# Backward state products by high and low parts, norm sums in two passes, four PSUM banks for the scan's products and one for the heads'

## The chip, the cores and the metric

One core of a Trainium2 chip. The time is that of one execution on the device, in microseconds; lower is better. The kernel before takes 2713.92 us (median of three runs, 2713.1 to 2715.24). All times below are of the kernel before.

## The reference

An encoder layer for two sequences, of 512 and 1024 tokens, laid end to end here as T = 1536. A normalised and modulated input `h` is multiplied by one wide matrix; one part of the result feeds an attention branch, the other a state-space scan that runs over the tokens in both directions; the two branches are gated, merged and projected. Everything is float32. What the change touches is the scan and the group norms:

```python
proj = h @ w_in                      # 1024 -> 8960
q = rms_norm(q_c, q_a_norm) @ w_q_up # q_c: 384 wide, kv_c: 256 wide
xbc = silu(dwconv_centred(xbc, conv_w, conv_b))
y = ssd(xs, dt_f, A_f, B, C) + flip(ssd(flip(xs), flip(dt_b), A_b, flip(B), flip(C)))
y = rms_norm_of_4_groups(y * silu(z), ssm_norm) @ w_proj_b
# ssd, per chunk of 128 tokens, 4 groups of 8 heads of 64:
y_diag = einsum(C B^T, decay between tokens, x * dt)
states = einsum(B, decay to the chunk's end, x * dt)     # 128 x 512 per group and chunk
h_next = exp(a_last) * h + states                        # over chunks, in both directions
y_off  = einsum(C, h, decay from the chunk's start)
```

## The kernel before

**Products in parts.** A product of float32 operands is made in one of two ways. Either both operands go to TensorE as they are ("fp32"; the trace then has two records for each instruction), or each operand is split in a high part (a cast to float32r on ScalarE) and a low part (the operand less its high part, on VectorE or GpSimd), and `mm3` (L87 to L90) runs three passes, high by high, high by low and low by high, added up in PSUM. The wide in-projection is made in this second way.

**Stages.** The input is normed and modulated (L165 to L261). Then a loop over the four groups g (L570 to L832): six convolution blocks (B, C and four of x: `conv_block`, each an in-projection block of three windows of 512 tokens, 24 products a window), the scan, and four blocks of z with the group's norm. After it come attention (L840 to L1140) and the output projections (L1143 to L1202).

**The scan of a group.** `prepass` goes backwards over a sequence's chunks: `tok` turns x and B to tokens by rows (five PE transposes, L588 and L590), `weighted` scales x by the decay (L598), one fp32 product makes the chunk's backward state (L626), `advance` adds it to the running state (L607, L609), which goes to DRAM (sbD, L628). `mainpass` goes forwards, two units of four heads to a chunk. For each chunk: `head` loads x and B back and the backward state and makes the chunk's C-B product (L651) and its two masked copies cu (L653, L654); `state` makes the high and low parts of the forward state's operands (L685 to L691; the low ones on GpSimd) and `follow` its product by `mm3` (L698); `carried` multiplies C with the states carried in (L677) and scales the result (L678); `decays` loads the decay rows (eb). For each unit: `distances` loads rows of cumulated decays (ab, from arD), `weights` subtracts on GpSimd (L714), makes scaled copies of cu on ScalarE (L718, L719) and adds and selects on VectorE (L720, L721), `weigh` multiplies (L727), `products` runs eight small products to one PSUM bank py per chunk (L738), and `tail` adds py to the output (L743, L744). The order over a chunk is written out in the loop at L756 to L776.

**What else runs there.** In-projection blocks that nothing in the scan needs ("fillers": latent q and k, gates) are fed between the scan's steps, 0.66 of a window to each step (L785 to L801). The backward sweep of the long sequence runs along with the forward pass of the short one.

**The norms.** `rms_cols` (L312) and `norm_qc` (L322) sum squares over the partitions by an fp32 product of the squares' sums with a matrix of ones (L315, L344; 12 and 6 of them) and make 1/sqrt by Ln and Exp (`rstd`, L92). `norm_x` (L183) has three more.

**Order.** The order of the work on each engine is made by the framework: it takes the instructions by the order of the program and by its own estimate of when each is ready, and hands out a pool's buffers in turn; each engine then runs its list in order. So a step that stands earlier in the code has a higher priority, not a fixed place. All DMAs are issued from SP, in order.

**PSUM.** Eight banks: three for in-projection products (`mmp`), three for all the scan's and norms' other products (`smp`, tiles `sm`), two for `py` (`yp`, L264).

Of the kernel before, what the change touches and what calls it, by code (L numbers as in the profile page):

```python
# [18 lines left out]
P = 128  # L19
# [46 lines left out]
def _body(nc, tc, A, O):  # L66
# [14 lines left out]
    def r32(ap):  # L81
        return ap.bitcast(F32)
# [27 lines left out]
    V.memset(ones, 1.0)  # L110
    epsc = const.tile([P, 1], F32, name="epsc")
# [46 lines left out]
    smp = pool("smp", bufs=3, space=PSUM)  # L158
# [105 lines left out]
    yp = pool("yp", bufs=2, space=PSUM)  # L264
# [46 lines left out]

    def rms_cols(tiles, gains, ss, n, w, dst):  # L312
        ws_ = slice(w * W, (w + 1) * W)
        ps = smp.tile([P, W], F32, name="sm")
        PE.matmul(ps, lhsT=ones, rhs=ss, start=True, stop=True)  # L315
        rs = tmp("zt")
        rstd(rs, ps, n)
        for t, g, d in zip(tiles, gains, dst):
            V.scalar_tensor_tensor(t[:, ws_], t[:, ws_], g, rs, op0=ALU.mult, op1=ALU.mult)
            nc.sync.dma_start(out=d[w], in_=t[:, ws_])  # L320

    def norm_qc():  # L322
# [19 lines left out]
        def scaled(w, js, ss, ts):  # L342
            ps = smp.tile([P, W], F32, name="sm")
            PE.matmul(ps, lhsT=ones, rhs=ss, start=True, stop=True)  # L344
            rstd(ss, ps, len(js) * P)
            for i, j in enumerate(js):
                V.scalar_tensor_tensor(ts[i], ts[i], col("kv_a" if len(js) == 2 else "q_a", i), ss, op0=ALU.mult, op1=ALU.mult)
                nc.sync.dma_start(out=qnT[j][w], in_=ts[i])
# [221 lines left out]
    for g in range(G):  # L570
# [40 lines left out]

        def prepass(o, n):

            c0, c1 = o // P, (o + n) // P
            st = None
            ahead = None
            for c in range(c1 - 1, c0 - 1, -1):
                now = None
                if c > c0:
                    xb = tok(c, "xp", 2)  # L620
                    nc.sync.dma_start(out=xbD[g][c], in_=xb)
                    now = (c, xb, weighted(xb[:, :W], 1, c))
                if ahead:
                    cc, xb, xd = ahead
                    ps = smp.tile([P, W], F32, name="sm")
                    PE.matmul(ps, lhsT=xb[:, W:], rhs=xd, start=True, stop=True)  # L626
                    st = advance(st, ps, 1, cc, p1.tile([P, W], F32, name="raw0", bufs=1) if st is None else st)
                    nc.sync.dma_start(out=sbD[g][cc - 1], in_=st)  # L628
                ahead = now
                yield  # L630

        def mainpass(o, n):
# [50 lines left out]
            def state(c):  # L683
                if c < c1 - 1:
                    xd = weighted(stt[c]["xt"], 0, c)  # L685
                    bh, bl = (pS.tile([P, P], F32R, name=n, bufs=1) for n in ("bth", "btl"))
                    xh, xl = (tmp("zt").bitcast(F32R) for _ in range(2))
                    S.copy(bh, stt[c]["bt"])  # L688
                    GP.tensor_tensor(bl, stt[c]["bt"], r32(bh), op=ALU.subtract)  # L689
                    S.copy(xh, xd)  # L690
                    GP.tensor_tensor(xl, xd, r32(xh), op=ALU.subtract)  # L691
                    stt[c]["parts"] = bh, bl, xh, xl
# [16 lines left out]
            def weights(c, u):  # L709
# [6 lines left out]
                t1 = pS.tile([P, HH, P], F32, name="t1", bufs=2)  # L716
# [39 lines left out]
            for i in range(len(us) + 1):  # L756
# [11 lines left out]
                if i + 1 < len(us):  # L768
                    weights(*us[i + 1])
                if i < len(us) and us[i][1] == 0:  # L770
                    c = us[i][0]
                    state(c)
                    decays(c)
                    if c + 1 < c1:
                        head(c + 1)
# [492 lines left out]
```

## Time and profile before

| what | value |
|---|---|
| median of three runs | 2713.92 us |
| profiled execution, its own time | 2716.42 us |
| its span, first to last instruction | 2714.4 us |
| mean granted TensorE clock | 0.985 |
| group loop, by the z blocks' and norms' ends | about 96 to 1599 us of the span |
| attention; output projections | to 2188 us; to the end |

The profiled execution is one run, so sums of its rows are held against 2716.42 us. Engines work at the same time, each through its own list in order. In rows of single instructions the bracket says how long the engine sat idle before it and what released it. A release by an instruction from which nothing is read is a wait for a buffer.

### The profile page before, as it was taken

The numbers are of one execution on the slowest core, as the hardware profiler recorded it, in microseconds if no ns is written. First come the engines' busy times: TensorE is split into PE (matmuls) and PEld (weight loads), VectorE is DVE, ScalarE is ACT, GpSimd is POOL, SyncE is SP. The second block draws the span as 40 slices with busy tenths as digits, with TensorE's granted clock in tenths as the row PEclk, the third lists the DMA queues.
The fourth block names the chain that finished last, engine by engine and source line by source line (L and its number), as shares of the span: only waits on it lengthen the run. The fifth ranks groups of instructions, "written<-read, shape, count | busy, mean of one in ns | idle before, by whom it ended". The sixth has DMA issues, their size and how long they took to land. (4 is left out here: it accounts for less than half of the span.)

```text
span 2714.4 us, 36314 instructions
## 1 busy us (share of the span) xinstructions
PE 2586.5 (95%) x12810; PEld 2080.5 (77%) x12810; DVE 1833.5 (68%) x2962; ACT 1322.6 (49%) x2954; POOL 505.1 (19%) x455
## 2 busy tenths in 40 slices
PE   6999999999999998999998999999999999999999
PEld 2776777877778766878766888888888788888887
DVE  5878785788946678557777568877777753466631
ACT  5545654456624456564556357666665651111210
POOL 1013440023400035110135024322222200000000
PEclk8999999999999999999999999999999999999999
DMA  7227662156722266542466322211110252255433
GB/s 249 77 78 208 187 168 94 39 179 187 207 62 86 82 208 183 136 147 74 146 191 188 92 96 87 84 44 43 34 40 28 71 186 70 78 156 163 128 125 101
DMA packets 211205, 325.86 MB, mean 120 GB/s; under 512 B 24816, under 2 KB 74064, under 8 KB 210256
## 3 DMA queue, kind: packets, MB, share of 16 engines
q1 hardware_dynamic: 211024, 323.55, 39.9%
q8 instruction: 101, 1.65, 0.3%
q14 instruction: 80, 0.66, 0.1%
HBM read 245.56 MB, written 77.91 MB: 119 GB/s over the span
## 5 line engine op out<-in xcount | busy, mean ns | idle before, releaser
L88 PE MATMUL mm<-hH,wh 128*128 128x512 f32 x1656 | 670.2, 405 | 2.3 <-ACT hH L218 2.0
L89 PE MATMUL mm<-hL,wh 128*128 128x512 f32 x1656 | 662.0, 400 | 3.6 <-DVE hL L219 3.6
L90 PE MATMUL mm<-hH,wl 128*128 128x512 f32 x1656 | 653.7, 395 | 1.3 <-DVE wl L85 1.2
L88 PEld LDWEIGHTS mm<-hH,wh 128*128 128x128 f32 x1656 | 314.6, 190 | 84.6 <-issue 14.6
L89 PEld LDWEIGHTS mm<-hL,wh 128*128 128x128 f32 x1656 | 315.4, 190 | 77.3 <-issue 10.2
L90 PEld LDWEIGHTS mm<-hH,wl 128*128 128x128 f32 x1656 | 314.6, 190 | 73.2 <-issue 6.1
L714 POOL TENSOR_TENSOR ab<-ab,dg 128x512 f32<-128x512 f32 x192 | 236.9, 1246 | 418.5 <-DMA ab<-arD 293.4
L88 PE MATMUL mm<-hi,wh 128*128 128x512 f32 x768 | 298.8, 389 | 0.0
L90 PE MATMUL mm<-hi,wl 128*128 128x512 f32 x768 | 298.8, 389 | 0.0
L89 PE MATMUL mm<-lo,wh 128*128 128x512 f32 x768 | 298.8, 389 | 0.0
L85 DVE TENSOR_TENSOR wl<-ws,wh 128x512 fp32r<-128x512 f32 x210 | 151.3, 722 | 134.4 <-ACT wh L226 86.7
L361 ACT CAST wh<-ws 128x512 fp32r<-128x512 f32 x72 | 44.9, 623 | 326.4 <-PE mm L89 311.3
L88 PEld LDWEIGHTS mm<-hi,wh 128*128 128x128 f32 x768 | 144.1, 188 | 30.1
L89 PEld LDWEIGHTS mm<-lo,wh 128*128 128x128 f32 x768 | 144.1, 188 | 29.9
L90 PEld LDWEIGHTS mm<-hi,wl 128*128 128x128 f32 x768 | 144.1, 188 | 29.9
L719 ACT ACTIVATE wt<-cu,dg 128x128 f32<-128x128 f32 x384 | 141.3, 391 | 46.5 <-DVE cu L653 46.1
L1025 ACT ACTIVATE pp<-sp,smx,rq 128x512 f32<-128x512 f32 x160 | 123.6, 777 | 54.9 <-DVE smx L1020 38.8
L361 ACT CAST ph<-tp 128x512 fp32r<-128x512 f32 x160 | 95.3, 598 | 110.4 <-PE tp L1059 110.2
L689 POOL TENSOR_TENSOR btl<-xb,bth 128x128 fp32r<-128x128 f32 x40 | 28.5, 713 | 607.5 <-ACT bth L688 607.4
L563 DVE SCALAR_TENSOR_TENSOR xs<-raw,cwh,xs 128x511 f32<-128x511 f32 (+3 forms) x128 | 129.7, 1021 | 17.5 <-ACT xs L559 14.8
L718 ACT ACTIVATE t<-cu,dg 128x128 f32<-128x128 f32 x384 | 137.3, 390 | 2.6 <-DVE cu L654 2.4
L721 DVE COPY_PREDICATED ab<-maskb,ab 128x512 f32<-128x512 uint8 x96 | 86.4, 905 | 69.3 <-POOL ab L714 69.3
(293 smaller groups left out, 5018.5 us busy)
## 6 DMA issues: line engine op xcount, KB each, us to landing
ab<-arD SPq DMA_DIRECT2D x192, 256.0 KB
ws<-w_in SPq DMA_DIRECT2D x140, 256.0 KB
eb<-arD SPq DMA_DIRECT2D x160, 128.0 KB
xbD<-xp SPq DMA_DIRECT2D x40, 320.0 KB
xb<-xbD SPq DMA_DIRECT2D x40, 320.0 KB
yT<-xs SPq DMA_DIRECT2D x48, 256.0 KB
sg<-yT SPq DMA_DIRECT2D x48, 256.0 KB
tg<-tga SPq DMA_DIRECT2D x48, 256.0 KB
```

Of the source, the lines that this page charges most:

```text
L85: V.tensor_tensor(out, a, b, op=ALU.subtract)
L88: PE.matmul(out, lhsT=ah, rhs=bh, start=first, stop=False)
L89: PE.matmul(out, lhsT=ah, rhs=bl, start=False, stop=False)
L90: PE.matmul(out, lhsT=al, rhs=bh, start=False, stop=last)
L361: S.copy(hi, src)
L563: V.scalar_tensor_tensor(acc[:, lo:hi], raw[:, lo + d:hi + d], cwh[:, 24 + 24 * k + tix:24 + 24 * k + tix + 1], acc[:, lo:hi], op0=ALU.mul ...
L689: GP.tensor_tensor(bl, stt[c]["bt"], r32(bh), op=ALU.subtract)
L714: GP.tensor_tensor(ab[:, d], ab[:, d], ac_[:, d, c, e0:e0 + HH].unsqueeze(2).broadcast_to([P, HH, P]), op=ALU.subtract)
L718: S.activation(t1[:, e], cu[:, 1, :], AF.Copy, scale=dt_[:, 1, c, e0 + e:e0 + e + 1])
L719: S.activation(wt[:, e], cu[:, 0, :], AF.Copy, scale=dt_[:, 0, c, e0 + e:e0 + e + 1])
L721: V.copy_predicated(ab[:, 0], maskb.unsqueeze(1).broadcast_to([P, HH, P]), ab[:, 1])
L1025: S.activation(pp[k], sps[k], AF.Exp, bias=sm[:, 2:3], scale=rq[:, b, h:h + 1], accum_out=st["su"][:, k, b:b + 1])
```

## The change

Five edits. The sums of the norms (`total`) are split in high and low part and multiplied with a float32r copy of the ones in two passes; the scale overwrites the sums' tile. The backward state's operands are split by the helper `split_state`, which the forward pass now uses too, and multiplied by `mm3`; in the backward sweep the low parts are made on VectorE, and the product stands before the next chunk's `tok`. The bank counts become `smp` 4 and `yp` 1. The tiles bth and btl get two buffers, t1 one. In the loop of `mainpass`, `state` and `decays` stand ahead of the next unit's `weights`.

```diff
+    onesr = const.tile([P, P], F32R, name="onesr")
+    S.copy(onesr, ones)
...
-    smp = pool("smp", bufs=3, space=PSUM)
+    smp = pool("smp", bufs=4, space=PSUM)
...
-    yp = pool("yp", bufs=2, space=PSUM)
+    yp = pool("yp", bufs=1, space=PSUM)
...
+    def total(ss, n):
+
+        ps = smp.tile([P, W], F32, name="sm")
+        hi, lo = (tmp("zt").bitcast(F32R) for _ in range(2))
+        S.copy(hi, ss)
+        sub(lo, ss, r32(hi))
+        PE.matmul(ps, lhsT=onesr, rhs=hi, start=True, stop=False)
+        PE.matmul(ps, lhsT=onesr, rhs=lo, start=False, stop=True)
+        rstd(ss, ps, n)
+
     def rms_cols(tiles, gains, ss, n, w, dst):
         ws_ = slice(w * W, (w + 1) * W)
-        ps = smp.tile([P, W], F32, name="sm")
-        PE.matmul(ps, lhsT=ones, rhs=ss, start=True, stop=True)
-        rs = tmp("zt")
-        rstd(rs, ps, n)
+        total(ss, n)
         for t, g, d in zip(tiles, gains, dst):
-            V.scalar_tensor_tensor(t[:, ws_], t[:, ws_], g, rs, op0=ALU.mult, op1=ALU.mult)
+            V.scalar_tensor_tensor(t[:, ws_], t[:, ws_], g, ss, op0=ALU.mult, op1=ALU.mult)
             nc.sync.dma_start(out=d[w], in_=t[:, ws_])
...
         def scaled(w, js, ss, ts):
-            ps = smp.tile([P, W], F32, name="sm")
-            PE.matmul(ps, lhsT=ones, rhs=ss, start=True, stop=True)
-            rstd(ss, ps, len(js) * P)
+            total(ss, len(js) * P)
...
+        def split_state(bt, xd, xh, xl, eng=GP):
+            bh, bl = (pS.tile([P, P], F32R, name=n, bufs=2) for n in ("bth", "btl"))
+            S.copy(bh, bt)
+            eng.tensor_tensor(bl, bt, r32(bh), op=ALU.subtract)
+            S.copy(xh, xd)
+            eng.tensor_tensor(xl, xd, r32(xh), op=ALU.subtract)
+            return bh, bl, xh, xl
+
         def prepass(o, n):
...
             for c in range(c1 - 1, c0 - 1, -1):
-                now = None
+                if ahead:
+                    cc, parts = ahead
+                    ps = smp.tile([P, W], F32, name="sm")
+                    mm3(ps, *parts, True, True)
+                    st = advance(st, ps, 1, cc, p1.tile([P, W], F32, name="raw0", bufs=1) if st is None else st)
+                    nc.sync.dma_start(out=sbD[g][cc - 1], in_=st)
                 if c > c0:
                     xb = tok(c, "xp", 2)
                     nc.sync.dma_start(out=xbD[g][c], in_=xb)
-                    now = (c, xb, weighted(xb[:, :W], 1, c))
-                if ahead:
-                    cc, xb, xd = ahead
-                    ps = smp.tile([P, W], F32, name="sm")
-                    PE.matmul(ps, lhsT=xb[:, W:], rhs=xd, start=True, stop=True)
-                    st = advance(st, ps, 1, cc, p1.tile([P, W], F32, name="raw0", bufs=1) if st is None else st)
-                    nc.sync.dma_start(out=sbD[g][cc - 1], in_=st)
-                ahead = now
+                    xd = weighted(xb[:, :W], 1, c)
+                    xr = p1.tile([P, 2 * W], F32, name="raw1", bufs=1).bitcast(F32R)
+                    ahead = c, split_state(xb[:, W:], xd, xr[:, :W], xr[:, W:], V)
                 yield
...
             def state(c):
                 if c < c1 - 1:
                     xd = weighted(stt[c]["xt"], 0, c)
-                    bh, bl = (pS.tile([P, P], F32R, name=n, bufs=1) for n in ("bth", "btl"))
-                    xh, xl = (tmp("zt").bitcast(F32R) for _ in range(2))
-                    S.copy(bh, stt[c]["bt"])
-                    GP.tensor_tensor(bl, stt[c]["bt"], r32(bh), op=ALU.subtract)
-                    S.copy(xh, xd)
-                    GP.tensor_tensor(xl, xd, r32(xh), op=ALU.subtract)
-                    stt[c]["parts"] = bh, bl, xh, xl
+                    stt[c]["parts"] = split_state(stt[c]["bt"], xd, *(tmp("zt").bitcast(F32R) for _ in range(2)))
...
-                t1 = pS.tile([P, HH, P], F32, name="t1", bufs=2)
+                t1 = pS.tile([P, HH, P], F32, name="t1", bufs=1)
...
-                if i + 1 < len(us):
-                    weights(*us[i + 1])
                 if i < len(us) and us[i][1] == 0:
                     c = us[i][0]
                     state(c)
                     decays(c)
+                if i + 1 < len(us):
+                    weights(*us[i + 1])
+                if i < len(us) and us[i][1] == 0:
                     if c + 1 < c1:
                         head(c + 1)
                 yield
```

## Rows read from the trace of the kernel before

**Rows 1.** The page's first part: busy us, share of span, instructions.

```profile
PE 2586.5 (95%) x12810; PEld 2080.5 (77%) x12810; DVE 1833.5 (68%) x2962; ACT 1322.6 (49%) x2954; POOL 505.1 (19%) x455
```

**Rows 2.** By stretch: length, PE, PEld, DVE, ACT, POOL busy, clock, DMA share, GB/s.

```profile
554.00:641.00 87.00, 83.32 (x432) 61.94 (x431) 70.98 (x105) 49.35 (x127) 26.39 (x22) 1.00 0.69 207
641.00:750.00 109.00, 99.65 (x554) 79.12 (x554) 97.44 (x139) 69.10 (x191) 55.66 (x46) 0.97 0.70 192
```

**Rows 3.** Waits of TensorE's matmuls: us in total, times, longest us.

```profile
PE sm L677 <- DVE cu L654: 21.8, 7, 4.8
...
PE sm L89 <- POOL zt L691: 14.3, 10, 3.2
PE sm L626 <- DVE eb L678: 9.0, 4, 3.4
...
PE sm L590 <- DVE eb L678: 4.5, 5, 1.3
```

**Rows 4.** Timeline of weight loads, one before each product, at round one's norm sums.

```profile
453.11 0.19 PEld L89 LDWEIGHTS mm<-hL,wh 128*128 128x128 f32 x1
453.34 0.19 PEld L90 LDWEIGHTS mm<-hH,wl 128*128 128x128 f32 x1
...
454.22 0.19 PEld L315 LDWEIGHTS sm<-eb,ones 128*128 128x128 f32 x1 [0.24 <-issue]
454.64 0.19 PEld L315 LDWEIGHTS sm<-eb,ones 128*128 128x128 f32 x1 [0.24 <-issue]
455.07 0.19 PEld L88 LDWEIGHTS mm<-hH,wh 128*128 128x128 f32 x1 [0.24 <-ACT zt L820]
```

**Rows 5.** Timeline of TensorE: a forward state product between fp32 products.

```profile
720.59 0.50 PE L88 MATMUL sm<-zt,bth 128*128 128x512 f32 x1
...
721.40 1.05 PE L677 MATMUL sm<-ch,stf 128*128 128x128 f32 x8
```

**Rows 6.** Timeline of all engines, 1070 to 1084 us: a burst in round three.

```profile
1070.00 3.48 POOL L714 TENSOR_TENSOR ab<-ab,dg 128x512 f32<-128x512 f32 x2 [6.96 <-DMA ab<-arD]
...
1070.32 0.66 PE L738 MATMUL py<-wt,xb 128*64 128x128 f32 x8
...
1071.33 0.66 PE L738 MATMUL py<-wt,xb 128*64 128x128 f32 x8
...
1073.85 1.71 POOL L691 TENSOR_TENSOR zt<-tmp,zt 128x512 fp32r<-128x512 f32 x1
...
1075.62 0.79 PE L89 MATMUL sm<-zt,bth 128*128 128x512 f32 x1 [3.20 <-POOL zt L691]
...
1078.04 1.55 DVE L721 COPY_PREDICATED ab<-maskb,ab 128x512 f32<-128x512 uint8 x1 [1.93 <-POOL ab L714]
...
1081.46 0.68 DVE L743 TENSOR_TENSOR eb<-eb,py 128x512 f32<-128x512 f32 x1
...
1082.86 0.28 DVE L654 TENSOR_TENSOR cu<-sm,cmat 128x128 f32<-128x128 f32 x1
...
1083.20 1.22 PE L677 MATMUL sm<-ch,sb 128*128 128x128 f32 x4 [4.38 <-DVE cu L654]
```

**Rows 7.** Timeline of all engines: the first of the 18 boundaries between chunks.

```profile
271.94 0.66 PE L738 MATMUL py<-wt,xb 128*64 128x128 f32 x8
...
273.18 0.68 DVE L743 TENSOR_TENSOR eb<-eb,py 128x512 f32<-128x512 f32 x1
```

**Rows 8.** Timeline of all engines: the last of the 18 boundaries between chunks.

```profile
1499.84 1.09 PE L738 MATMUL py<-wt,xb 128*64 128x128 f32 x16
...
1501.33 0.68 DVE L743 TENSOR_TENSOR eb<-eb,py 128x512 f32<-128x512 f32 x1
```

**Rows 9.** Groups by line, shapes apart: busy us, mean ns, idle before, releaser.

```profile
L85 DVE TENSOR_TENSOR wl<-ws,wh 128x512 fp32r<-128x512 f32 x210 | 151.3, 722 | 134.4 <-ACT wh L226 86.7 <-ACT wh L361 39.5 <-PE sm L588 8.1
...
L598 DVE TENSOR_TENSOR tmp<-xp,dg 128x512 f32<-128x512 f32 x40 | 38.9, 973 | 3.1 <-PE sm L626 2.0 <-ACT xp L592 1.1
...
L690 ACT CAST zt<-tmp 128x512 fp32r<-128x512 f32 x40 | 24.6, 616 | 19.6 <-DVE tmp L598 19.6
```

## The prediction

> **What bounds the kernel now.** I read the busy shares first: TensorE is busy 2586.5 us of a span of 2714.4 [rows 1], so a microsecond taken out of TensorE's queue is worth about one, wherever the queue has work. The kernel has four equal rounds (one per state group). In each of them six convolution blocks and four z blocks keep TensorE full; between them lies the scan, an early half (backward sweep and the short sequence) and a late half (the long sequence). The change touches the scan and the norms at each round's end.
>
> Next, the busy times by stretch. In round two the early half lasts 87 us and the late half 109 us [rows 2]. VectorE is busy 71 and 97 us of these, 82% and 89%, with a granted clock of 1.00 and 0.97. So in the scan TensorE is not alone: VectorE is nearly as full, and it works in order, so one late input holds up all behind it.
>
> Then the waits of TensorE [rows 3]. Seven waits, 21.8 us, are of the carried products (L677) for the mask product L654: L677 takes nothing from L654; it wants the PSUM bank that L654 still reads. The waits for L678 (9.0 and 4.5 us) are of that kind too. Another 14.3 us are waits of the state product's second pass (L89) for the low part that GpSimd makes at L691.
>
> One burst shows how both arise [rows 6]. GpSimd has waited 6.96 us for distances (ab) to land; then it does two L714 in 3.48 us, and only then the low part, 1.71 us from 1073.85. TensorE stands 3.20 us for it. VectorE's L721 is released late by GpSimd as well, L743 and L654 stand behind it, and TensorE stands another 4.38 us at 1083.20 until L654 has left its bank.
>
> **The change part by part.** The sum is made against the profiled execution, 2716.4 us; the median of the runs is 2713.9, 2.5 us less.
>
> Norm sums (18 of the 21 products against ones; L183's three stay). An fp32 product of 128x512 takes two records 0.42 to 0.43 us apart, so 0.86 us; the one-pass form takes 0.23 us [rows 4]. Two passes are 0.46: saved 0.40 x 18 = **-7.3 us**, among blocks that keep TensorE full. Added are 18 casts (0.62) and 18 subtractions (0.72 by the same subtraction of weights, 0.97 by the slowest alike) [rows 9], 11 us on ScalarE and 13 to 17 on VectorE. They cost nothing while in-projection or convolution products cover them: a chain of 1.3 to 1.6 us is put ahead of each sum, and blocks of 24 products (24 x 0.23 = 5.4 us) stand beside it. With that cover gone 18 x 1.6 = 29 us would be open. The scale now overwrites the sums' tile, so the two zt buffers serve the high and low part.
>
> Backward state products (40). Before, one fp32 product, 0.86 us. After, three passes: 0.69 by the 0.23 us step, 0.81 by the forward state's own three between fp32 neighbours (from 720.59 to the next at 721.40) [rows 5]. Saved 0.05 to 0.17 each, 2 to 7 us; the forward's is the same operation in the same place, but not all neighbours are fp32: **-4 us**. Added per chunk: two casts on ScalarE and two subtractions on VectorE (128x512 and 128x128). The large pair is 0.62 and 0.72 to 0.97 us [rows 9]; the small one, a quarter as wide, I set at half at most. So 40 x (0.72 to 1.5) = 29 to 60 us of VectorE, 10 chunks in each round, 7 to 15 us, in an early half where VectorE has 16 us free [rows 2]. This is the thinnest cover of the change. No more than a part can come through: **+5 us**, between 0 and 15. The product now stands ahead of the next chunk's transposes instead of behind them; its parts are made an iteration earlier, and its DMA (state out) moves along on SP's queue, past that chunk's copy out. I cost that at nothing, since both write to memory and nobody in that iteration reads them.
>
> Four banks for the scan's products (smp 3 to 4). The bank that L677 takes is then one product older, read by VectorE long before. Behind each of the seven L654 waits a block product is queued that has all it needs, so all 21.8 us go; what is late next is the block's evacuation. Of the other bank waits (9.0 and 4.5 [rows 3]) I take two thirds, as VectorE gets fuller there: together **-31 us**, between 0 and -35.
>
> State ahead of weights. On GpSimd the two state subtractions now go before the two L714; on ScalarE two casts go before eight scalings; on VectorE L598 goes before L720 and L721. SP issues are not passed: the eb loads of the decays already stood between the ab and head loads, and weights issue no DMA. In the burst the low part would come 3.48 us earlier and the wait of 3.20 go [rows 6]. Over all, 14.3 us of such waits [rows 3], of which I take **-10**. Against it L714 of the next unit comes up to 1.71 us plus the small subtraction later, and L721, L743 and all behind with it: **+5**, between 0 and 40 x 0.5.
>
> Clock. The late half runs at 0.97 [rows 2], 3 us of full-speed work short in 109, part of it idle anyway. Fewer long waits: **-5 us** over four rounds, between 0 and -10.
>
> One bank for the heads' products (yp 2 to 1). New wait: the first products of chunk c+1 (L738) may not start until L743 has read chunk c's. In the burst, chunk c's products are at 1070.32, the next at 1071.33, and L743 runs at 1081.46: with this order alone TensorE would stand 10.9 us there [rows 6]. I set L738 against L743 at all 44 boundaries inside a round: in 18 the next products begin before L743 has ended, the first at 271.94 against 273.18 to 273.86 [rows 7], the last in the run of 16 records from 1499.84 against 1501.33 to 2.01 [rows 8]; 74 us in sum. In the other 26 a filler block (5.4 us) lies between. Behind the waiting L738 stand the carried products, the state product and the next block. The price lies between 0 (the scheduler orders engines by its own estimate, and can put block products in the gap and L743 forward) and 74; I take **+15**, near the lower end, since a wait here and the waits at L677 and L89 in the same burst are one lateness of VectorE and can't all be paid.
>
> The rest: one buffer for t1 makes ScalarE's scalings wait for L720 of the unit before; bth and btl get two buffers, which the two sweeps share; one more constant is cast once. ScalarE is busy 69 of 109 us in the late half [rows 2], so these are free; if L720 stood behind a late L721 they would add to the same lateness.
>
> Sum: -7.3 - 4 + 5 - 31 - 10 + 5 - 5 + 15 = -32. 2716.4 - 32 = 2684, or 2682 against the median's level.
>
> A rule of the Trainium skill speaks against the last part: Perfetto Trace Analysis, Matmuls, says that independent groups of products should go round several PSUM banks, so that reading out one overlaps the products of the next. By it the single heads' bank costs its read-out at every boundary, 44 x 0.68 = 30 us at most by L743's own length, and the sum would be 2697; the trace has a read-out of 0.68 us, but 26 boundaries have a block between.
>
> **Rivals.** *The heads' bank takes over the waits* (slower). Place: L738 at the 18 boundaries without a block between. It decides where L743 still runs over 0.7 us after the products it reads. Price: 74 less 18 x 0.7 for block products put in the gap, 61; the waits on L654 and L691 (36 us) and about 8 of the other bank waits fall away, as VectorE has caught up by then: +17. With -11 for the cheaper products and +10 for fuller engines: +16, so 2730. For it: the recorded lags; against it: the scheduler sees the new dependence.
>
> *VectorE becomes the bound* (about no change). Early halves grow by the added 7 to 15 us less the 16 free, and the late half is 89% full already. What banks give is then idle time on TensorE: -11 for the products, -10 for waits, +18 on VectorE, 2711. For: [rows 2]. Against: the late halves get no added VectorE work.
>
> *All waits go*: -7 - 7 - 35 - 14 - 10 = -73, 2641 at the median's level.
>
> **How the numbers follow.** Forecast case 0.55, heads' bank 0.23, VectorE 0.15, all waits 0.07. The forecast case by itself runs from 2660 to 2704 (heads' bank 0 to +30, bank waits by 10 either way). The range takes in most of both neighbours: 2652 to 2731. A measurement of this kernel can tell 0.2%, 5.4 us, from no change. Faster: nearly all of the forecast case, the last one, and little else, 0.62; within: 0.13, most of the VectorE case; slower: 0.25.
>
> **What would show it.** Right: no L677 waits on L654, L89 waits on L691 under 5 us, 18 pairs of sums at 0.23 us a pass, and TensorE's waits in the scan under half. The heads' bank rival shows as L738 waiting for L743, some 18 times, up to 10 us. The VectorE rival shows as an early half over 92% VectorE at an unchanged length. I am wrong if the late halves do not shorten, or if convolution or z stretches lengthen, where sums only save.

## The result: 32 us slower

| | before | after |
|---|---|---|
| median, same chip | 2713.51 us | 2745.85 us |
| ratio, 95% interval | | 1.0113 [1.009, 1.0136] |
| profiled execution; its span | 2716.42; 2714.4 us | 2744.21; 2742.3 us |
| mean granted TensorE clock | 0.985 | 0.981 |

The forecast was 2682 us, 2652 to 2731: wrong in sign, and outside the range. Lines have moved: after's L747, L752, L669, L692, L723, L730, L623 and L624 are before's L738, L743, L654, L677, L714, L721, L690 and L691 (the last two now serve both sweeps).

The busy times of after, as [rows 1]:

```profile
PE 2588.2 (94%) x12850; PEld 2094.0 (76%) x12850; DVE 1893.3 (69%) x3060; ACT 1369.0 (50%) x3053; POOL 516.8 (19%) x455
```

VectorE has 98 instructions and 60 us more; TensorE's busy time has not fallen, though it now has the cheaper products. Round two by stretch, columns as in [rows 2], early and late half:

```profile
561.00:651.00 90.00, 84.09 (x441) 64.96 (x440) 79.98 (x124) 56.28 (x144) 28.71 (x21) 0.98 0.63 189
651.00:764.00 113.00, 100.12 (x552) 79.77 (x551) 101.13 (x140) 71.23 (x194) 55.62 (x48) 0.94 0.70 194
```

Early 87 to 90 us, late 109 to 113: both longer. The same view over all eight halves of the four rounds (from a round's first transpose to its last head product) ends in a sum; its first figure is their length. Before, then after:

```profile
sum 779.10, PE 713.89 PEld 549.71 DVE 626.14 ACT 470.47 POOL 301.62; mean PE 89.24 PEld 68.71 DVE 78.27 ACT 58.81 POOL 37.70
```

```profile
sum 800.30, PE 718.68 PEld 564.29 DVE 676.15 ACT 506.20 POOL 314.51; mean PE 89.83 PEld 70.54 DVE 84.52 ACT 63.28 POOL 39.31
```

So 21 of the profiled 28 us are in the scan; the rest shows up around the norms, below. TensorE's waits in after, as in [rows 3]:

```profile
PE py L747 <- DVE eb L752: 36.7, 10, 7.0
...
PE sm L88 <- ACT raw L623: 14.6, 12, 4.6
PE sm L89 <- POOL zt L624: 9.1, 8, 1.9
PE sm L320 <- ACT zt L318: 7.0, 7, 1.4
PE sm L89 <- DVE raw L624: 6.6, 10, 1.4
...
PE mm L88 <- ACT raw L555: 4.6, 1, 4.6
```

The row of the carried products waiting for L654's bank (21.8 us) is gone, as forecast. In its place stand 36.7 us of the heads' products for the read-out of their one bank, 14.6 and 6.6 us for the backward parts (raw), and 7.0 us for the parts of the norm sums. The longest heads' wait, on the timeline of after:

```profile
1089.36 4.11 POOL L723 TENSOR_TENSOR ab<-ab,dg 128x512 f32<-128x512 f32 x3 [3.02 <-DMA ab<-arD]
1090.43 0.73 DVE L730 COPY_PREDICATED ab<-maskb,ab 128x512 f32<-128x512 uint8 x1 [2.94 <-POOL ab L723]
...
1093.94 0.71 DVE L730 COPY_PREDICATED ab<-maskb,ab 128x512 f32<-128x512 uint8 x1
...
1094.56 0.67 DVE L752 TENSOR_TENSOR eb<-eb,py 128x512 f32<-128x512 f32 x1
...
1095.28 1.12 PE L747 MATMUL py<-wt,xb 128*64 128x128 f32 x8 [7.04 <-DVE eb L752]
```

It is the burst of [rows 6] over again: distances land late, GpSimd and then VectorE are late, and TensorE stands, now at the heads' bank.

### The profile page after: what moved, and what is told of

Same layout as the page of the kernel before. It is cut to its first block, busy times and chain, and to the rows that moved or that the text cites. A ratio compares the mean times of both kernels' runs of the same rounds, so it can differ in the third digit from the quotient of the medians.

```text
span 2742.3 us, 36606 instructions
## 1 busy us (share of the span) xinstructions
PE 2588.2 (94%) x12850; PEld 2094.0 (76%) x12850; DVE 1893.3 (69%) x3060; ACT 1369.0 (50%) x3053; POOL 516.8 (19%) x455
## 5 line engine op out<-in xcount | busy, mean ns | idle before, releaser
L88 PE MATMUL mm<-hH,wh 128*128 128x512 f32 x1656 | 662.5, 400 | 8.4 <-ACT raw L555 4.6
L90 PE MATMUL mm<-hH,wl 128*128 128x512 f32 x1656 | 652.7, 394 | 3.2 <-DVE wl L85 3.2
L89 PE MATMUL mm<-hL,wh 128*128 128x512 f32 x1656 | 651.7, 394 | 2.3 <-DVE hL L221 2.3
L88 PEld LDWEIGHTS mm<-hH,wh 128*128 128x128 f32 x1656 | 314.9, 190 | 84.6 <-issue 8.5
L90 PEld LDWEIGHTS mm<-hH,wl 128*128 128x128 f32 x1656 | 314.0, 190 | 71.0 <-DVE wl L85 4.1
L89 PEld LDWEIGHTS mm<-hL,wh 128*128 128x128 f32 x1656 | 314.6, 190 | 68.9 <-DVE hL L221 4.4
L723 POOL TENSOR_TENSOR ab<-ab,dg 128x512 f32<-128x512 f32 x192 | 239.0, 1257 | 425.1 <-DMA ab<-arD 179.8
L88 PE MATMUL mm<-hi,wh 128*128 128x512 f32 x768 | 298.8, 389 | 0.0
L90 PE MATMUL mm<-hi,wl 128*128 128x512 f32 x768 | 298.8, 389 | 0.0
L89 PE MATMUL mm<-lo,wh 128*128 128x512 f32 x768 | 298.8, 389 | 0.0
L85 DVE TENSOR_TENSOR wl<-ws,wh 128x512 fp32r<-128x512 f32 x210 | 150.3, 718 | 127.1 <-ACT wh L228 79.2
L368 ACT CAST wh<-ws 128x512 fp32r<-128x512 f32 x72 | 44.9, 623 | 323.8 <-PE mm L89 311.3
L88 PEld LDWEIGHTS mm<-hi,wh 128*128 128x128 f32 x768 | 144.1, 188 | 30.1
L90 PEld LDWEIGHTS mm<-hi,wl 128*128 128x128 f32 x768 | 144.1, 188 | 29.9
L89 PEld LDWEIGHTS mm<-lo,wh 128*128 128x128 f32 x768 | 144.1, 188 | 29.9
L728 ACT ACTIVATE wt<-cu,dg 128x128 f32<-128x128 f32 x384 | 141.1, 391 | 38.4 <-DVE cu L668 38.3
L622 POOL TENSOR_TENSOR btl<-xb,bth 128x128 fp32r<-128x128 f32 x40 | 34.6, 866 | 632.0 <-ACT bth L621 515.1
L727 ACT ACTIVATE t<-cu,dg 128x128 f32<-128x128 f32 x384 | 136.9, 390 | 16.1 <-DVE wt L729 13.7
L228 ACT CAST wh<-ws 128x512 fp32r<-128x512 f32 x138 | 84.7, 616 | 108.1 <-PE mm L89 94.4
```

The lines of the kernel that those rows point to most:

```text
L85: V.tensor_tensor(out, a, b, op=ALU.subtract)
L88: PE.matmul(out, lhsT=ah, rhs=bh, start=first, stop=False)
L89: PE.matmul(out, lhsT=ah, rhs=bl, start=False, stop=False)
L90: PE.matmul(out, lhsT=al, rhs=bh, start=False, stop=last)
L228: S.copy(a, ws)
L368: S.copy(hi, src)
```

## The experiments

Each ran beside the kernel before, whose median lay between 2711.35 and 2714.28 us; a difference is always against that of the same runs. Single executions of one kernel spread by up to 0.7%, so a stage of one trace is read for its large terms only. "Halves" is the sum just shown (before 779); t1 alone, free by its median, reads 788 in its one trace.

| | median us | ratio to before, 95% | difference | halves |
|---|---|---|---|---|
| banks alone | 2722.22 | 1.0036 [1.0019, 1.0053] | +7.9 | 788 |
| backward parts alone | 2729.57 | 1.0061 [1.0039, 1.0083] | +15.3 | 803 |
| norm sums alone | 2721.57 | 1.0033 [1.0016, 1.005] | +7.3 | 777 |
| order alone | 2722.35 | 1.0034 [1.0016, 1.0052] | +8.1 | 792 |
| one heads' bank alone | 2725.39 | 1.0048 [1.0025, 1.0071] | +11.8 | 790 |
| fourth bank from blocks | 2716.71 | 1.001 [0.9999, 1.0022] | +3.1 | 771 |
| the same, with order | 2720.87 | 1.0028 [1.0017, 1.0039] | +8.0 | 777 |
| whole, banks as before | 2745.84 | 1.0125 [1.011, 1.014] | +32.9 | 802 |
| whole, no backward parts | 2734.5 | 1.0075 [1.0059, 1.0091] | +20.9 | 790 |
| parts, product late | 2735.07 | 1.0074 [1.0056, 1.0092] | +21.4 | 800 |
| parts, all low on GpSimd | 2751.2 | 1.0143 [1.0126, 1.016] | +38.3 | 821 |
| t1 alone | 2713.9 | 1.0002 [0.9988, 1.0016] | +1.0 | 788 |
| parts made, not used | 2732.43 | 1.0086 [1.0069, 1.0104] | +20.6 | 801 |
| parts, all low on VectorE | 2717.59 | 1.0023 [1.0008, 1.0037] | +5.7 | 787 |
| before, forward low on VectorE | 2699.57 | 0.996 [0.9945, 0.9975] | -12.3 | 763 |
| group norms' sums alone | 2722.07 | 1.0052 [1.0033, 1.0072] | +10.2 | 784 |
| whole, forward low on VectorE | 2731.88 | 1.0067 [1.0041, 1.0093] | +20.5 | 787 |
| forward low on VectorE, fourth bank from blocks | 2696.95 | 0.9946 [0.9926, 0.9965] | -14.4 | 761 |

### Each part by itself

The theories: A, the heads' single bank carries the loss; B, the backward states' parts do; C, the norm sums do.

```diff
-    smp = pool("smp", bufs=3, space=PSUM)
+    smp = pool("smp", bufs=4, space=PSUM)
-    yp = pool("yp", bufs=2, space=PSUM)
+    yp = pool("yp", bufs=1, space=PSUM)
```

> The kernel before with the bank counts alone changed (smp 4, yp 1). Theory A (the heads' single bank carries the loss: L738 waits for L743 wherever VectorE is late): 2730 to 2745 us, L738 waiting for L743 30 to 60 us, the waits of L677 on L654 (21.8 us before) gone. Theory B (the loss comes from the backward state's longer chain of casts and subtractions): the fourth bank helps by itself, 2690 to 2708 us, L738 waiting for L743 under 10 us. Theory C (the norms' split sums lose it): as B.

The other three take the hunks of the change shown above: `split_state`, `prepass` and the buffer counts; `total` and its two callers; the loop of `mainpass`.

> The kernel before with the backward states' products by parts alone (and what they need: two buffers of bth and btl, one of t1, the product ahead of the next chunk's transposes). Theory A: 2705 to 2715 us, the extra work hidden. Theory B: 2725 to 2740 us, with TensorE waiting 15 to 25 us for the casts and the subtractions of the backward state, and early halves longer by 2 to 5 us in each round. Theory C: as A.

> The kernel before with the norms' sums in two passes alone. Theories A and B: 18 x 0.40 us less on TensorE, 2704 to 2710 us. Theory C (the products stand and wait for the high part, 9 us, and what is late behind them, 5 us): 2716 to 2722 us.

> The kernel before with state and decays ahead of the next unit's weights alone. All theories: the waits of L89 for L691 (14.3 us) fall to 4 to 9 us, 2703 to 2712 us. If the later L714 costs as much as the earlier L691 gives, 2712 to 2720 us, with the waits of L677 on L654 above 25 us.

All four cost: 7.9 + 15.3 + 7.3 + 8.1 = 38.6 us, and the whole 32. No theory alone was right: the backward parts came as B had them and the norm sums as C had them, the banks lie between the ranges, and the order lies above both of its ranges. TensorE's waits with the banks alone, and with the order alone:

```profile
PE py L738 <- DVE eb L743: 33.3, 14, 5.2
...
PE sm L89 <- POOL zt L691: 12.9, 11, 2.6
```

```profile
PE sm L677 <- DVE cu L654: 26.7, 8, 6.3
...
PE sm L651 <- DVE stf L609: 7.5, 5, 2.8
```

With the banks, 21.8 us of L654 become 33.3 of L743. With the order, L89's 14.3 us for L691 fall to 4.0 as meant, but L654's grow from 21.8 to 26.7 and the C-B product stands 7.5 us, before 1.9 (single traces: with t1 alone L654's row is 17.8, with the group norms' sums 23.3). For the norm sums alone, the weight loads where [rows 4] had two L315 records at the step of their neighbours:

```profile
464.26 0.19 PEld L89 LDWEIGHTS mm<-hL,wh 128*128 128x128 f32 x1
465.79 0.19 PEld L320 LDWEIGHTS sm<-zt,onesr 128*128 128x128 f32 x1 [1.34 <-ACT zt L318]
465.89 0.19 PEld L90 LDWEIGHTS mm<-hH,wl 128*128 128x128 f32 x1
...
470.25 0.19 PEld L88 LDWEIGHTS mm<-hH,wh 128*128 128x128 f32 x1
470.79 0.19 PEld L321 LDWEIGHTS sm<-zt,onesr 128*128 128x128 f32 x1 [0.35 <-DVE zt L85]
```

A pass is placed among block products just before its part is ready: from 464.26 to 465.79 instead of 0.23 us for one step.

### What the banks are worth

```diff
-    yp = pool("yp", bufs=2, space=PSUM)
+    yp = pool("yp", bufs=1, space=PSUM)
```

> The kernel before with one bank for the heads' products instead of two and nothing else (the scan's other products keep three banks, one bank stays empty). It prices the heads' bank alone. A (the single heads' bank brings a new wait, and the fourth bank for the others takes some of it back): the products wait for the output's addition (L743) some 30 to 40 us in sum, the waits of the carried products for the mask product (L654) partly stay, and the time is 2730 to 2745 us, above the 2722 of the banks together. B (the wait only takes the place of waits that are there anyway, so the fourth bank bought nothing): the waits for L654 shrink without the fourth bank too, and the time is 2718 to 2726, as with both.

The heads' bank alone costs 11.8 us, with 28.4 us of L738 for L743. B held: the time is in its range, and L677's row for L654 is gone although there is no fourth bank. With the fourth bank it was 7.9: that bank gave back 3.9, not 31, and as the two intervals overlap, not even the 3.9 is clear of noise. The opposite edit keeps the heads' two banks:

```diff
-    mmp = pool("mmp", bufs=3, space=PSUM)
-    smp = pool("smp", bufs=3, space=PSUM)
+    mmp = pool("mmp", bufs=2, space=PSUM)
+    smp = pool("smp", bufs=4, space=PSUM)
```

> The kernel before with four banks for the scan's products, two for the heads' as before, and the bank taken from the in-projection blocks instead (three to two). A (a fourth bank is worth the waits that it removes when the heads keep their two): the waits of L677 for L654 go, no L738 waits for L743, and the time is 2690 to 2708 us, unless the blocks pay for their two banks; that would show as waits of L88 for the evacuations in the convolution and z stretches. B (the waits are one lateness of VectorE that turns up at whatever product comes next): L677 no longer waits for L654, but waits of about the same sum stand at other products of the late halves, and the time is 2710 to 2722. C (two banks are too few for the blocks): over 2725, with conv and z stretches longer by 2 us or more each.

```profile
PE sm L89 <- POOL zt L691: 36.2, 20, 5.0
```

No row of L677 for L654, and none of L738 for L743; but L89 for L691 is 36.2 us where it was 14.3 [rows 3]. The 21.8 us did not go, they moved: 14.3 + 21.8 = 36.1. Added up from the traces over the eight halves, TensorE's idle times of over 0.15 us are 64.8 us before and 64.8 here. B held. That the blocks' lost bank hides a gain is not excluded: L88 stands 5.0 us once for the block's copy L548, which it does not do before. Next this together with the order, which takes away L89's wait:

> The kernel before with four banks for the scan's products (the bank taken from the in-projection blocks, three to two) and with state and decays ahead of the next unit's weights. The banks in this form alone were at 2716.7 us, 3 above before, with no wait of L677 for L654 and 36 us of waits of L89 for L691; the order alone was at 2722.4, with 4 us of L89 for L691 and 27 of L677 for L654: each takes away the wait that the other leaves. A (the waits are causes of their own): both go, and the time is 2685 to 2700 us. B (they are one lateness of the scan's own chain, and stand at whichever product comes next): both rows are under 15 us, the waits of TensorE in the scan's halves stay at 55 to 70 us in sum, at other products, and the time is 2712 to 2724.

L89 for L691 is 4.8 us, and now L90 waits 22.0 us for low parts of weights (L85) and L738 14.4 for L727. B again: the wait goes to the next product that needs VectorE, and the halves' idle times are 65.9 us. Last, the whole change with the bank counts of before:

> The whole change with the bank counts of before (three for the scan's other products, two for the heads'). Its 36.7 us of waits of the heads' products for the output's addition must go. A (the heads' bank carries its part of the loss in the whole, too): 2728 to 2738 us. B (the same lateness then shows at the mask product's bank): 25 us or more of waits of L677 (here L669's reader) for the mask product come back and the time is 2739 to 2750. Under 2728 the banks would be the main cause of the loss, against the sum of the parts alone.

2745.84 us, +32.9 beside the whole's +32.3: in company the banks cost nothing and give nothing. The 36.7 us at the heads' bank are gone, and 28.2 us of L692 for L669 are there again. B held.

### What the backward parts cost

First the product's place: behind the next chunk's transposes, as before.

```diff
                 if c > c0:
                     xb = tok(c, "xp", 2)
...
                 if ahead:
...
+                    mm3(ps, *parts, True, True)
...
+                if c > c0:
+                    xr = p1.tile([P, 2 * W], F32, name="raw1", bufs=1).bitcast(F32R)
+                    now = c, split_state(xb[:, W:], xd, xr[:, :W], xr[:, W:], V)
```

> The change's backward states by parts alone, but with the product left where it was, behind the next chunk's transposes. With the product moved ahead this alone was at 2729.57 us, 15 above the kernel before. A (the place is the cost: the product follows its low part too closely): waits of L88 and L89 for L616, L617 fall below 12 us together, early halves are within 2 us of before, and the time is 2712 to 2719. B (the added operations on VectorE and ScalarE are the cost, wherever the product stands): early halves stay 4 us or more above before each, and the time is 2725 to 2732. In between would say that both count.

The waits for backward parts fell as A said (7.2 us for the casts), yet the time rose to 2735, above both ranges: the forward product's waits for GpSimd's low part went to 38.7 us and L654's bank's to 23.6. Then the engine, in the version with the product ahead, and the buffer count:

```diff
-                    ahead = c, split_state(xb[:, W:], xd, xr[:, :W], xr[:, W:], V)
+                    ahead = c, split_state(xb[:, W:], xd, xr[:, :W], xr[:, W:], GP)
```

> Backward states by parts alone, as in the run that was at 2729.57 us, but with the backward low parts made on GpSimd instead of VectorE. A (the work added to a nearly full VectorE is the cost): the early halves are within 3 us of before and the time is 2714 to 2722 us. B (the longer chain from x by rows to the low part is the cost, on whichever engine; GpSimd takes 1.7 us for what VectorE does in about 1): waits of L88 and L89 for the parts grow above 45 us and the time is 2730 to 2745.

```diff
-                t1 = pS.tile([P, HH, P], F32, name="t1", bufs=2)
+                t1 = pS.tile([P, HH, P], F32, name="t1", bufs=1)
```

> The kernel before with one buffer for t1 instead of two and nothing else. It tells whether the buffer counts that came along with the backward parts carry some of their 15 us. A (free, as forecast): 2711 to 2717 us, waits as before. B (ScalarE's scalings wait for L720 and make the heads late): 2719 to 2730, with late halves 1 to 3 us longer each and the early ones unchanged.

t1 is free. With all low parts on GpSimd it is 2751.2 us, the slowest of all, with 32.4 us of waits for the backward low parts alone; B, but above its range. Its early half of round two, columns as in [rows 2]:

```profile
566.80:667.10 100.30, 86.61 (x435) 66.28 (x434) 78.97 (x104) 56.90 (x146) 48.71 (x42) 0.95 0.60 181
```

GpSimd has 20 instructions more, VectorE none (104, before 105), and yet VectorE is busy 79 us instead of 71 [rows 2]. That points to the two engines slowing each other. To tell work from chain, the next kernel makes all the parts and uses none of them; the fp32 product stays:

```diff
-                    now = (c, xb, weighted(xb[:, :W], 1, c))
+                    xd = weighted(xb[:, :W], 1, c)
+                    now = (c, xb, xd)
...
+                    S.copy(bh, xb[:, W:])
+                    V.tensor_tensor(bl, xb[:, W:], r32(bh), op=ALU.subtract)
+                    S.copy(xr[:, :W], xd)
+                    V.tensor_tensor(xr[:, W:], xd, r32(xr[:, :W]), op=ALU.subtract)
```

> The kernel before, with its one fp32 product of the backward state where it was, and with the casts and subtractions of the change made beside it on ScalarE and VectorE into tiles that nobody reads (t1 keeps one buffer, to make room). It adds the split's work without its chain. A (the added work on engines that run in order is enough: what stands behind it comes later): 2724 to 2732 us, early halves 4 us or more longer each. B (only the longer way from x by rows to the product costs): 2710 to 2718, early halves within 2 us of before.

2732.43 us, +20.6: A by its time, at the upper edge; the early halves, though, grew by 4.1, 0.6 and 5.9 us (in round two the border between the halves moved), not by 4 each. Nobody waits for these parts, so the work by itself costs 20.6: 80 casts on ScalarE and 80 subtractions on VectorE, which this run does not tell apart. With the parts used and the product in the same place it was +21.4, so a gain of the cheaper products is not to be seen; the +15.3 with the product ahead is lower, but the intervals overlap. In its waits, L89 for GpSimd's forward low part has grown from 14.3 to 22.2 us. Then the forward low parts go to VectorE as well, first with the backward parts, then on the kernel before:

```diff
-                    stt[c]["parts"] = split_state(stt[c]["bt"], xd, *(tmp("zt").bitcast(F32R) for _ in range(2)))
+                    stt[c]["parts"] = split_state(stt[c]["bt"], xd, *(tmp("zt").bitcast(F32R) for _ in range(2)), V)
```

> Backward states by parts alone, as in the run at 2729.57 us, but with the forward low parts on VectorE as well, so that GpSimd makes no low parts at all. In the run with all low parts on GpSimd (2751.2) VectorE's busy time in an early half grew by about 10 us though it had no operation more than before: the two engines slow each other. A (that slowing and GpSimd's 1.6 us a low part are a good part of the cost): 2712 to 2723 us, fewer waits of L89, L598 and L607 nearer 0.7 us. B (VectorE's queue is the cost, and 40 more low parts on it make it longer): 2732 to 2748.

```diff
-                    GP.tensor_tensor(bl, stt[c]["bt"], r32(bh), op=ALU.subtract)
+                    V.tensor_tensor(bl, stt[c]["bt"], r32(bh), op=ALU.subtract)
...
-                    GP.tensor_tensor(xl, xd, r32(xh), op=ALU.subtract)
+                    V.tensor_tensor(xl, xd, r32(xh), op=ALU.subtract)
```

> The kernel before with the forward state's low parts made on VectorE instead of GpSimd, nothing else. Its 14.3 us of waits of L89 for L691 must go. A (GpSimd's slow low part is a cause of its own): 2696 to 2708 us. B (one lateness: VectorE gets 40 x 1 us more to do in order and the waits stand elsewhere): 2710 to 2722, with more than 21.8 us of waits of L677 for L654. C (VectorE becomes the bound in the late halves): above 2722.

2717.59 and 2699.57 us, both in A's ranges. The second is faster than both kernels of this case. But of these two, run side by side, the one with the backward parts is 18.0 us slower: they cost as much without GpSimd's low parts as with them (15.3). So GpSimd's low part is a cost that the kernel before has too, and not what made the change lose. The first part of the second one's page, and its rows by group:

```profile
PE 2581.0 (96%) x12810; PEld 2077.5 (77%) x12810; DVE 1834.4 (68%) x3042; ACT 1321.4 (49%) x2954; POOL 411.0 (15%) x375
```

```profile
L598 DVE TENSOR_TENSOR tmp<-xp,dg 128x512 f32<-128x512 f32 x40 | 33.0, 824 | 1.2 <-ACT xp L592 1.1
...
L691 DVE TENSOR_TENSOR zt<-tmp,zt 128x512 fp32r<-128x512 f32 x40 | 31.7, 792 | 0.6 <-ACT zt L690 0.6
...
L609 DVE TENSOR_TENSOR raw<-raw,sm 128x512 f32<-128x512 f32 x32 | 21.7, 677 | 0.3
```

And the low part's row before:

```profile
L691 POOL TENSOR_TENSOR zt<-tmp,zt 128x512 fp32r<-128x512 f32 x40 | 63.6, 1591 | 63.6 <-ACT zt L690 63.6
```

VectorE does 80 instructions more in the same time (1834.4 us, before 1833.5 [rows 1]). The low part takes it 0.79 us on average; GpSimd took 1.59. L598 falls from 973 to 824 ns [rows 9]. The waits for L691 go from 14.3 to 5.1 us and those for L654 from 21.8 to 5.3. Three things come together in this edit and were not tried apart: GpSimd's list is shorter, the low part is made faster, and the two engines slow each other less.

How the two engines meet shows on the timeline of the kernel with the backward parts alone:

```profile
603.06 0.67 DVE L598 TENSOR_TENSOR tmp<-xb,dg 128x512 f32<-128x512 f32 x1
...
603.88 1.04 POOL L716 TENSOR_TENSOR ab<-ab,dg 128x512 f32<-128x512 f32 x1 [2.87 <-DVE tmp L598]
...
604.05 1.42 DVE L607 TENSOR_TENSOR raw<-raw,dg 128x512 f32<-128x512 f32 x1
...
604.88 1.72 POOL L617 TENSOR_TENSOR zt<-tmp,zt 128x512 fp32r<-128x512 f32 x1
...
605.39 1.76 DVE L598 TENSOR_TENSOR tmp<-xp,dg 128x512 f32<-128x512 f32 x1
...
607.08 0.68 DVE L609 TENSOR_TENSOR raw<-raw,sm 128x512 f32<-128x512 f32 x1
607.18 0.62 ACT L616 CAST raw<-tmp 128x512 fp32r<-128x512 f32 x1 [1.38 <-DVE tmp L598]
...
608.39 1.04 POOL L716 TENSOR_TENSOR ab<-ab,dg 128x512 f32<-128x512 f32 x1 [1.78 <-DMA ab<-arD]
608.47 1.50 DVE L617 TENSOR_TENSOR raw<-tmp,raw 128x512 fp32r<-128x512 f32 x1
```

The same L598 takes 0.67 us alone and 1.76 beside GpSimd's L617. Each of the slowed ones ends about one undisturbed length after the other engine's end: L607 at 605.47, 0.55 after GpSimd's at 604.92; GpSimd's L617 at 606.60, 1.13 after L607's; L598 at 607.15, 0.55 after that. L609 takes one input from PSUM and is not slowed; beside GpSimd, in the trace of the kernel before:

```profile
705.80 1.08 POOL L714 TENSOR_TENSOR ab<-ab,dg 128x512 f32<-128x512 f32 x1 [2.96 <-DMA ab<-arD]
...
706.11 0.67 DVE L609 TENSOR_TENSOR stf<-stf,sm 128x512 f32<-128x512 f32 x1
```

Counted over that trace, 30 of the 64 L609 run beside a GpSimd instruction, and none of the 64 takes more than 0.71 us. Of the 80 L598 the 55 alone take at most 0.71 too, and the 25 beside GpSimd 1.21 on average and up to 1.78. This is what the Trainium skill says (SBUF — State Buffer, Who interferes with whom): a VectorE instruction with two SBUF inputs contends with a GpSimd instruction that reads SBUF, for ports that only one of the two can hold at a time, and the order of issue decides who is blocked. The rows agree, and the late cast at 607.18 (1.38 us idle for L598) shows how one meeting moves down the chain.

### The whole change again

Without the backward parts, their place and buffer counts; then the whole with the forward low parts on VectorE, the one word `V` as above.

> The whole change without its backward states by parts, their move and their buffer counts: banks, order and norm sums stay. The four parts alone cost 8, 15, 7 and 8 us, 38 in sum, the whole 32. A (the parts' costs add up): 2728 to 2733 us. B (the scan's parts meet in one lateness, and where one is gone another pays): 2738 to 2746. C (the banks and the order help as soon as the early half carries no more than before): 2715 to 2724.

> The whole change with one word added: the forward state's low parts on VectorE instead of GpSimd. On the kernel before this gave 14 us, on the backward parts alone 12. A (the added work in the scan and the slowing by GpSimd carry most of the loss, in the whole too): 2727 to 2736 us, early halves within 4 us of before each, waits of the heads' products for the output's addition fewer than 36.7 us. B (with the heads' one bank and the norm sums in it, the gain is taken by other waits): 2737 to 2748.

2734.5 us, between the ranges and nearer to A: the backward parts are 11.4 us of the whole's 32.3. 2731.88 us: with the word the whole is at +20.5 instead of +32.3, in A's range, and the waits at the heads' bank fall from 36.7 to 19.9 us with no bank added, while those for the backward casts (L88 for L623) rise from 14.6 to 26.2. The early halves are 92.3, 94.8, 92.6 and 93.6 us where before had 88.8, 86.1, 91.2 and 87.1, two of them over the 4 us that A allowed: the backward work remains. The word gives about 12 us here and 12.3 on the kernel before. So the change costs as much (20.5 + 12.3 = 32.8) on a kernel without GpSimd's low parts: their slowing isn't seen to carry any of its loss.

### The norm sums once more

`total` stays in `rms_cols`; the latent norms (`scaled`) keep their fp32 product.

> The norm sums in two passes alone, but only the 12 of the group norms; the 6 of the latent norms stay one fp32 product each. With all 18 it was 2721.57 us, 5 us of which stood in the convolution stretch of round four, at one wait of 4.6 us for a copy of raw. A (that wait comes from the latent norms' later end, which holds the tile that the convolution's copy wants): the wait is gone and the time is 2711 to 2717 us. B (it comes from the group norms): the wait stays and the time is 2718 to 2722.

Neither: the wait of 4.6 us for raw is gone, as A said, and the time is 2722.07 us, as B said. So that wait isn't the cost. The traces show where the time is. With the norm sums alone the passes wait 6.3 us for L318 and 1.6 for L85; these 7.9 us take up what was to be saved. The stretch between the scans of rounds three and four is 188.2 us long, before 184.7 (187.2 in this run, without the wait for raw). And the attention's start, from its first product to its first transpose, takes 38.6 us, before 34.6. TensorE's wait there, before, then with the norm sums alone:

```profile
PE sp L88 <- ACT wqh L361: 1.4, 1, 1.4
```

```profile
PE sp L88 <- ACT wqh L368: 3.9, 1, 3.9
```

ScalarE's cast of wqh stands behind a copy that waits 4.9 us, before 2.4, for a gate's store (tgb) to land; that store is issued behind the last norm's four stores, which come later now. All six kernels with two-pass group sums show this wait at 3.5 to 5.4 us, 13 of the other 14 at 1.4 (the fourth bank with the order: 3.5). That these two places carry the loss is read from the traces, not tried.

### Forward low parts on VectorE, and a fourth bank

> The kernel before with the forward low parts on VectorE (alone 2699.57 us) and four banks for the scan's other products, the bank taken from the in-projection blocks (alone 2716.7). A (with the lateness of GpSimd gone, the fourth bank is worth the 5.3 us of waits for the mask product and some of the 7.7 for L678 that are left): 2688 to 2696 us. B (these waits too only move): 2697 to 2703. C (two banks are too few for the blocks once the scan is faster): above 2703.

2696.95 us, the fastest median, between the ranges of A and B; its interval overlaps that without the fourth bank, so the bank is not shown to add anything. Here L654's row is gone too, and L738 stands 10.6 us for L727 and L590 9.0 for L609.

## Why the prediction was wrong

**Four banks, -31: the step that failed most.** "All 21.8 us go" took a wait in [rows 3] for a cause. The waits went from the bank, and came up at L691, L85, L727 or L743, whichever product next needed VectorE or GpSimd; measured -3.9 beside the heads' one bank, not clear of noise, and +3.1 with the bank taken from the blocks. The burst [rows 6] had been read rightly as one lateness, and the prediction used that to keep the heads' bank cheap, but not against its own gains.

**Backward work, +5 between 0 and 15: mis-sized.** It measured +20.6 as work alone. Its amount was right: the 60 us more on VectorE, for 98 instructions, lie within the prediction's own 42 to 77 (29 to 60 here, 13 to 17 at the norms). Its cover was wrong. It was said to be VectorE's 16 free us of an early half; but on an engine that runs its list in order, added work makes what stands behind it later, wherever the free time is. That the work costs is shown. That it does so by the subtractions in front of L598, L743 and the low parts, and not by the casts on ScalarE, is argued from the order and not tried. The gain of the products, -4, is not to be seen in the runs.

**State ahead of weights, -10 + 5: wrong sign.** The -10 came out in its row (14.3 to 4.0), but the whole is +8.1 alone and 4.9 on top of the fourth bank (8.0 less 3.1). That L714 comes later, and L654 and L743 with it, at more than the +5, is the likely path: L654's row grew, by little more than single traces differ. The path was not tried apart.

**One heads' bank, +15: right within its bounds.** +11.8 alone. The rule of the Trainium skill that was weighed there (Perfetto Trace Analysis, Matmuls: rotate banks; from it the estimate of 30 at most) agrees with that run, and its 28.4 us of waits. In company the bank costs nothing (+32.9 without it, +32.3 with it).

**Norm sums, -7.3: wrong.** +7.3. "They cost nothing while block products cover them" asked whether there is work beside the chain, not where in TensorE's queue the passes are put: ahead of the parts, so the queue stands at them, 7.9 us for the 7.3 saved. And it left out what follows the norm: a store that the attention's start waits for comes later, and the stretch before round four's scan is longer.

**Clock, -5: wrong sign.** The granted clock has two levels, 1.2 and 2.4 GHz, so the time at the lower one is 2 x (1 - mean) x span: before 81 us, after 104, with the parts made and not used 115 (mean 0.979), with the forward low parts on VectorE 70 (0.987). It rose with the idle time; which of the two brought the other is not shown. At half speed, 23 us more cost at most 11.5, an estimate.

The rival of the heads' bank came nearest (2730), with its row there as described, at 10 places and not 18; but its reason falls with the run at 2745.84 without that bank. The VectorE rival had the place (early halves) and priced it by free time, the same mistake; VectorE reached 89% there, not 92. Three readings of the prediction are a little off, and none moves the sum: 24 x 0.23 is 5.5, the wait in the burst is 10.8 by its rows, and the 18 boundaries give 72.

## What to carry to other kernels

When several waits of one engine start from the same late neighbour, removing one of them (a bank, a place in the order) is worth about nothing until the neighbour is earlier; look for the latest instruction in the burst and who slows it. Price added work on an in-order engine by what stands behind it, not by the engine's idle share; making the work without using it is a cheap test. Before splitting element-wise work between VectorE and GpSimd, compare the same line's duration alone and beside the other engine: here moving 80 subtractions off GpSimd cost VectorE nothing and gave 12 us, to the kernel before as to the changed one.

## What was not expected of the hardware

That the exchange is nearly free: VectorE's busy time was 1833.5 us without and 1834.4 with the 80 extra subtractions, while GpSimd's fell from 505.1 to 411.0. And that a 128x512 subtraction with both inputs in SBUF goes from 0.67 to 1.76 us beside GpSimd, while an addition with one input in PSUM stays within 0.71.
